# Up projection: products on TensorE, and casts and subtractions of left forms, chained in program order

## The chip, the cores and the metric

The kernel runs on one core of a Trainium2 chip. The metric is the device time of one execution in microseconds (us). The engines are named as in the profile: PE is TensorE, DVE is VectorE, ACT is ScalarE, POOL is GpSimd, and SP is the engine that issues most transfers.

## The reference

One layer of a decoder trunk with 1024 tokens and a model width of 1024. Only its last part, the gated MLP, touches the change:

```
def conv_gated_ffn(h, w_up, conv_w, conv_b, w_down):
    u, v = jnp.split(h @ w_up, 2, axis=-1)
    u = lax.conv_general_dilated(u, conv_w[:, None, :], window_strides=(1,),
                                 padding=[(CONV_W - 1, 0)], ...) + conv_b
    return (jax.nn.silu(u) * v) @ w_down
```

`h` is the normalised activation (1024 x 1024), `w_up` is 1024 x 5632, so `u` and `v` have 2816 columns each; the convolution along the tokens is causal and has width 3. All data are float32.

## The kernel before

The product `h @ w_up` is computed by tiles of 128 columns. Tile f of `u` and tile f of `v` (f = 0 to 21) make one **pair**. Within a pair the kernel uses a scheme of seven products in place of eight: the two column tiles, the two halves of the inner dimension (512 each) and the two halves of the tokens (512 each) make a 2 x 2 block product, done as Winograd's variant of Strassen's scheme. The left factors are weights or sums of weights (A11, A12, A22 and S1 to S4, called **left forms**), the right factors are activations or sums of them (B11, B21, B22 and T1 to T4), made once in `trunk`.

Each product is computed in split precision. A factor is held as a high part, cast to a reduced format, and a low part, the difference. `left` makes a form: POOL adds weights where the form is a sum (L1308), ACT casts the high part (L1315), and DVE and POOL in turn subtract for the low part (L1316). The form's tile has one of two tags in turn, with two buffers each, so the cast of a form can run only when the product four forms earlier has ended. `prod` issues the product: twelve matmuls of 128 x 512, for each of four inner blocks high x high, high x low, low x high (L1323).

In a pair, the products accumulate into a bank a (`ps_a`), a bank b (`ps_b2`, in the profile `ps_b`), and one tile `cd` of two banks (`ps_cd`), whose halves are c and d. In the code's order: A11 x B11 into a, S2 x T2 into b, S3 x T3 into c, S1 x T1 into d, A12 x B21 into a, A22 x T4 into c, S4 x B22 into d. DVE adds the partial sums as they come (L1384 u2 = b + s1, L1386 u3 = c + u2, L1388 the second half of vt = d + u3, L1393 the first half of vt = c + u2, L1395 the second half of u = d + u2), and then convolution, silu and the gate follow, called the y chain here: L1397 on ACT, L1398 and L1399 on DVE, the silu L1400 on ACT, L1401 on DVE, and then L1404 (even f) or L1411 (odd f) on DVE. PSUM holds two `ps_cd` tiles, one `ps_b` for each of two pairs, and two `ps_a`.

For the first six pairs the two products into bank a are computed ahead, by `ahead`, and their results are kept in DRAM (`part_dram`); these pairs have five products left. `ahead` starts while `trunk` still transposes activations, so that the first products stand among the transposes (L1254) of the last token blocks and the token-major matmuls (L1099).

The order of instructions on each engine is set by a scheduler, which works from dependencies and a timing estimate of its own. Where the code demands no order, two products, of one pair or of two neighbouring pairs, may be interleaved. `tc.issue_after(x)` adds the demand that what is issued inside it stands behind instruction x.

Of the kernel before, what the change touches and what calls it, by code (L numbers as in the profile page):

```python
# [12 lines left out]
F32 = mybir.dt.float32  # L13
# [4 lines left out]
ALU = mybir.AluOpType  # L18
# [78 lines left out]
class K:  # L97
# [1197 lines left out]
    def left(self, r1, r2, which, sp):  # L1295

        nc = self.nc
        V, A, G = nc.vector, nc.scalar, nc.gpsimd
        q = {f"A{n}{k + 1}": r[:, 4 * k:4 * k + 4, :] for n, r in ((1, r1), (2, r2)) if r is not None for k in range(2)}
        sums = {"S1": ("A21", "A22", ALU.add), "S2": ("S1", "A11", ALU.subtract), "S3": ("A11", "A21", ALU.subtract),  # L1300
                "S4": ("A12", "S2", ALU.subtract)}

        def get(n):
            if n not in q:
                a, b, op = sums[n]
                a, b = get(a), get(b)
                q[n] = sp.tile([P, 4, P], F32, tag=n, name=n, bufs=2 if n in ("S1", "S2") else 1)
                G.tensor_tensor(out=q[n], in0=a, in1=b, op=op)  # L1308
            return q[n]

        for n in which:
            x = get(n)
            self.nform = getattr(self, "nform", 0) + 1
            f = self.wp.tile([P, 2, 4, P], F32R, tag=("whi", "wlo")[self.nform % 2], name="wf")
            A.copy(out=f[:, 0], in_=x)  # L1315
            (V if self.nform % 2 else G).tensor_tensor(out=f[:, 1], in0=x, in1=f[:, 0].bitcast(F32), op=ALU.subtract)  # L1316
            yield f

    def prod(self, ps, f, x, start, stop):
        n = 0  # L1320
        for k in range(4):
            for a, b in ((0, 0), (0, 1), (1, 0)):
                self.nc.tensor.matmul(ps, lhsT=f[:, a, k, :], rhs=x[b][:, k, :], start=(start and n == 0), stop=(stop and n == 11),  # L1323
                                      skip_group_check=not start)
                n += 1

    def ffn_up(self, X, act, sums, part, spill):

# [302 lines left out]
```

## Time and profile before

| | us |
|---|---|
| time, median of 3 runs | 2422.68 |
| its lowest and highest run | 2419.61, 2427.7 |
| the profiled execution's own time | 2418.76 |
| its span | 2417.0 |
| PE busy in the span | 2312.8 (96%) |
| DVE busy | 1373.9 (57%) |
| ACT busy | 908.9 (38%) |
| POOL busy | 695.2 (29%) |

The span runs from the first to the last instruction of the profiled execution, 1.8 us less than its time. Positions in the rows are microseconds from the start of the span. The up projection's products lie between 1700 and 2192 us. The busy time of an engine counts time in which it works on an instruction, waits not included; the wait in brackets behind a row of the timeline is the idle time of the engine just before the instruction, with what ended it.

### The profile page before, as it was taken

Reading aid. Unit: us, or ns where it says so; the run is one execution under the profiler, and the core shown is the slowest. Engines: PE = TensorE matmul, PEld = TensorE weight load, DVE = VectorE, ACT = ScalarE, POOL = GpSimd, SP = SyncE. Lnnn points to the kernel's source line nnn. Section 1 sums busy time; section 2 is a strip of 40 time slices with the busy share of each in tenths; the row PEclk is TensorE's granted clock in tenths of the full one; section 3 lists DMA queues with packets and bytes.
Section 4 is the critical chain, followed back from the end, with each engine's and each line's share of the span. In section 5 each row is a group of like instructions: output and inputs, shape, how many; then the busy total and the mean of one; then the engine's idle time right before and its main releaser. Section 6 shows DMA issues by size and latency. Waiting matters only on the chain. (4 is left out here: it accounts for less than half of the span.)

```text
span 2417.0 us, 34889 instructions
## 1 busy us (share of the span) xinstructions
PE 2312.8 (96%) x13988; PEld 1887.5 (78%) x13988; DVE 1373.9 (57%) x2098; ACT 908.9 (38%) x1430; POOL 695.2 (29%) x580
## 2 busy tenths in 40 slices
PE   7999999899999999999999999999898999998998
PEld 7877768686778787888878778888676888886886
DVE  6446374757424557454564464545547656667775
ACT  6542213131314435344442233443333333334443
POOL 1011001010111333333132440141456666551041
PEclk9999999999999999999999999999999999999999
DMA  8653312121222111111103662224243322238333
GB/s 302 221 176 125 92 58 97 58 92 45 76 70 81 53 53 37 35 60 54 44 27 121 215 213 96 96 88 135 106 165 135 111 94 105 105 142 306 97 96 122
DMA packets 110930, 266.14 MB, mean 110 GB/s; under 512 B 27248, under 2 KB 31984, under 8 KB 110768
## 3 DMA queue, kind: packets, MB, share of 16 engines
q1 hardware_dynamic: 108656, 258.25, 31.9%
q0 software_dynamic: 1248, 4.46, 0.5%
q8 instruction: 110, 1.80, 0.3%
q10 hardware_dynamic: 864, 1.20, 0.1%
q14 instruction: 52, 0.43, 0.1%
HBM read 194.40 MB, written 69.47 MB: 109 GB/s over the span
## 5 line engine op out<-in xcount | busy, mean ns | idle before, releaser
L155 PE MATMUL ps_d<-hThi,whi 128*128 128x512 f32 x1056 | 425.9, 404 | 2.0 <-DVE Ktt L261 1.6
L157 PE MATMUL ps_d<-hTlo,whi 128*128 128x512 f32 x1056 | 424.2, 402 | 0.0
L159 PE MATMUL ps_d<-hThi,wlo 128*128 128x512 f32 x1056 | 424.1, 402 | 0.0
L140 ACT CAST whi<-raw 128x1024 fp32r<-128x1024 f32 (+1 forms) x170 | 167.2, 989 | 331.4 <-PE ps_d L157 155.4
L143 DVE TENSOR_TENSOR wlo<-raw,whi 128x1024 fp32r<-128x1024 f32 (+1 forms) x125 | 156.9, 1262 | 138.2 <-ACT whi L140 138.2
L155 PEld LDWEIGHTS ps_d<-hThi,whi 128*128 128x128 f32 x1056 | 199.9, 189 | 44.5 <-issue 3.2
L157 PEld LDWEIGHTS ps_d<-hTlo,whi 128*128 128x128 f32 x1056 | 199.9, 189 | 42.8 <-issue 4.6
L159 PEld LDWEIGHTS ps_d<-hThi,wlo 128*128 128x128 f32 x1056 | 199.7, 189 | 42.7 <-issue 4.2
L143 POOL TENSOR_TENSOR wlo<-raw,whi 128x1024 fp32r<-128x1024 f32 (+1 forms) x45 | 96.8, 2150 | 433.1 <-ACT whi L140 388.4
L1490 PE MATMUL ps_dn<-wd,ap 128*128 128x512 f32 x924 | 213.2, 393 | 7.1 <-ACT wd L1466 6.7
L1490 PEld LDWEIGHTS ps_dn<-wd,ap 128*128 128x128 f32 x924 | 175.1, 190 | 45.2 <-ACT wd L1466 7.1
L1315 ACT CAST wf<-S 128x512 fp32r<-128x512 f32 x88 | 54.7, 622 | 165.0 <-PE ps_cd L1323 76.5
L1466 ACT CAST ap<-acr 128x512 fp32r<-128x512 f32 x77 | 47.9, 623 | 104.2 <-PE ps_dn L1490 93.2
L1467 DVE TENSOR_TENSOR ap<-acr,ap 128x512 fp32r<-128x512 f32 x77 | 61.4, 799 | 41.4 <-ACT ap L1466 40.6
L745 DVE CUSTOM_DVE_ANT_0 a_p<-ps_s,a_bias 128x512 f32<-128x512 f32 (+3 forms) x96 | 51.7, 553 | 50.3 <-PE ps_s L743 45.0
L159 PE MATMUL ps_d<-ohi,wlo 128*128 128x512 f32 x192 | 75.9, 395 | 3.3 <-DVE wlo L143 3.3
L1316 POOL TENSOR_TENSOR wf<-S,wf 128x512 fp32r<-128x512 f32 x44 | 62.0, 1409 | 56.1 <-ACT wf L1315 56.1
L755 ACT ACTIVATE a_p<-a_p,a_nm 128x128 f32<-128x128 f32 (+7 forms) x64 | 49.2, 770 | 75.2 <-POOL a_nm L751 57.8
L157 PE MATMUL ps_d<-olo,whi 128*128 128x512 f32 x192 | 75.8, 395 | 0.0
L155 PE MATMUL ps_d<-ohi,whi 128*128 128x512 f32 x192 | 75.8, 395 | 0.0
L1113 POOL TENSOR_SCALAR ms<-ms 128x1 f32<-128x1 f32 x30 | 11.1, 371 | 224.0 <-ACT xn L1112 146.1
L1308 POOL TENSOR_TENSOR S<-raw 128x512 f32<-128x512 f32 x44 | 58.9, 1341 | 35.6 <-DVE wf L1316 21.8
(436 smaller groups left out, 5386.3 us busy)
## 6 DMA issues: line engine op xcount, KB each, us to landing
raw<-t_in SPq DMA_DIRECT2D x66, 512.0 KB, 3.6
raw<-t_up SPq DMA_DIRECT2D x50, 512.0 KB, 3.5
th_dram<-th SPq DMA_DIRECT2D x24, 512.0 KB, 2.8
mth<-th_dram SPq DMA_DIRECT2D x24, 512.0 KB, 3.7
wdr<-ffn_w_down SPq DMA_DIRECT2D x44, 256.0 KB, 5.2
acr<-act_dram SPq DMA_DIRECT2D x44, 256.0 KB, 2.7
act_dram<-y SPq DMA_DIRECT2D x20, 512.0 KB, 2.6
acr<-sums_dram SPq DMA_DIRECT2D x33, 256.0 KB, 2.6
```

Source lines behind the costliest of these rows:

```text
L140: nc.scalar.copy(out=hi, in_=raw)
L143: eng.tensor_tensor(out=lo, in0=raw, in1=hi.bitcast(F32), op=ALU.subtract)
L155: nc.tensor.matmul(o, lhsT=hi[:, k, :], rhs=xhi(k, h), start=(k == 0), stop=False)
L157: nc.tensor.matmul(o, lhsT=hi[:, k, :], rhs=xlo(k, h), start=False, stop=False)
L159: nc.tensor.matmul(o, lhsT=lo[:, k, :], rhs=xhi(k, h), start=False, stop=(k == nk - 1))
L745: V.tensor_tensor_reduce(out=p_[:, a:b], in0=ps[:, 0:b - a], in1=bias[:, 1024 - n + a:1024 - n + b], op0=ALU.add, op1=ALU.max, scale=1.0, ...
L755: A.activation(out=pr[c][:, 0:n], in_=pr[c][:, 0:n], func=AF.Exp, bias=nm[:, c:c + 1], accum_out=Z[:, c:c + 1])
L1308: G.tensor_tensor(out=q[n], in0=a, in1=b, op=op)
L1315: A.copy(out=f[:, 0], in_=x)
L1316: (V if self.nform % 2 else G).tensor_tensor(out=f[:, 1], in0=x, in1=f[:, 0].bitcast(F32), op=ALU.subtract)
L1467: V.tensor_tensor(out=t[:, 1], in0=z, in1=t[:, 0].bitcast(F32), op=ALU.subtract)
L1490: T.matmul(ps[t], lhsT=a[:, p, P * t:P * t + P], rhs=w[:, q, :], start=(not behind and j == 0 and n == 0), stop=(j == NJ - 1 and n == 2), ...
```

## The change

`prod` now issues all its twelve matmuls behind the last matmul of the product that the code issued before it, over all calls, so that products on PE stand in the code's order and none is interleaved with another. A new function `inorder` chains instructions of one kind: the casts of left forms on ACT ("A"), the subtractions on DVE (1) and those on POOL (0). The instructions themselves stay as they were. Lines of the changed kernel behind the edit carry higher numbers: the cast is L1316, the subtraction L1317, the matmuls L1332, and each line from L1338 of the old numbering on is 12 higher.

```diff
--- before.py
+++ after.py
@@ -1312,17 +1312,29 @@
             x = get(n)
             self.nform = getattr(self, "nform", 0) + 1
             f = self.wp.tile([P, 2, 4, P], F32R, tag=("whi", "wlo")[self.nform % 2], name="wf")
-            A.copy(out=f[:, 0], in_=x)
-            (V if self.nform % 2 else G).tensor_tensor(out=f[:, 1], in0=x, in1=f[:, 0].bitcast(F32), op=ALU.subtract)
+            e = self.nform % 2
+            self.inorder("A", lambda: A.copy(out=f[:, 0], in_=x))
+            self.inorder(e, lambda: (G, V)[e].tensor_tensor(out=f[:, 1], in0=x, in1=f[:, 0].bitcast(F32), op=ALU.subtract))
             yield f
 
+    def inorder(self, n, f):
+
+        last = self.__dict__.setdefault("kinds", {})
+        with self.tc.issue_after(last[n].ins) if n in last else ExitStack():
+            last[n] = f()
+
     def prod(self, ps, f, x, start, stop):
-        n = 0
-        for k in range(4):
-            for a, b in ((0, 0), (0, 1), (1, 0)):
-                self.nc.tensor.matmul(ps, lhsT=f[:, a, k, :], rhs=x[b][:, k, :], start=(start and n == 0), stop=(stop and n == 11),
-                                      skip_group_check=not start)
-                n += 1
+
+        with self.tc.issue_after(self.before) if self.before is not None else ExitStack():
+            n = 0
+            for k in range(4):
+                for a, b in ((0, 0), (0, 1), (1, 0)):
+                    i = self.nc.tensor.matmul(ps, lhsT=f[:, a, k, :], rhs=x[b][:, k, :], start=(start and n == 0),
+                                              stop=(stop and n == 11), skip_group_check=not start)
+                    n += 1
+        self.before = i.ins
+
+    before = None
 
     def ffn_up(self, X, act, sums, part, spill):
```

The first place is PE in one pair of seven products, whose tile is `ps_cd_16159`. These are rows of the order before; `ps_cd_16298`, `ps_b2_16297` and `ps_a_16278` belong to the next pair, and what stands in brackets is which engines the matmul waits for.

```order
L1323 MATMUL ps_cd_16159<-T3hi_14291,wf_16184 128x512
...
L1323 MATMUL ps_a_16139<-B21hi_13803,wf_16216 128x512 [waits Activation_49]
...
L1323 MATMUL ps_cd_16159<-T1hi_14150,wf_16200 128x512 [waits DVE_49]
...
L1323 MATMUL ps_b2_16297<-T2hi_14141,wf_16305 128x512 [waits Activation_49]
...
L1323 MATMUL ps_a_16278<-B11hi_13794,wf_16279 128x512 [waits Activation_49]
...
L1323 MATMUL ps_cd_16159<-T4hi_14159,wf_16232 128x512 [waits DVE_49]
...
L1323 MATMUL ps_cd_16298<-T3hi_14291,wf_16323 128x512 [waits Activation_49]
L1323 MATMUL ps_cd_16298<-T3lo_14292,wf_16323 128x512
L1323 MATMUL ps_cd_16159<-B22hi_14321,wf_16250 128x512 [waits DVE_49]
```

And these are the rows of the changed order for the same pair.

```order
L1332 MATMUL ps_cd_16159<-T3hi_14291,wf_16184 128x512
L1332 MATMUL ps_cd_16159<-T1hi_14150,wf_16200 128x512 [waits DVE_49,Activation_49]
...
L1332 MATMUL ps_a_16139<-B21hi_13803,wf_16216 128x512 [waits Activation_49]
...
L1332 MATMUL ps_cd_16159<-T4hi_14159,wf_16232 128x512 [waits DVE_49,Activation_49]
...
L1332 MATMUL ps_cd_16159<-T4hi_14159,wf_16232 128x512
L1332 MATMUL ps_cd_16159<-B22hi_14321,wf_16250 128x512 [waits DVE_49,Activation_49]
...
L1332 MATMUL ps_a_16278<-B11hi_13794,wf_16279 128x512 [waits Activation_49]
```

T1 stood behind B21 and now stands right behind T3; B22 stood behind products of the next pair and now stands right behind T4, and B21 has moved between T1 and T4.

The second place is DVE around the addition u3 of the same pair (L1386); `y_16119` and `vt_16010` belong to the pair before. First the order before.

```order
L1395 TENSOR_TENSOR u_14365<-ps_cd_16012,u2_16013 128x512
L1384 TENSOR_TENSOR u2_16160<-ps_b2_16158,s1_16155 128x512
L1398 SCALAR_TENSOR_TENSOR y_16119<-u_14365,par_70,y_16119 128x1024
L1386 TENSOR_TENSOR u3_16161<-ps_cd_16159,u2_16160 128x512
L1316 TENSOR_TENSOR wf_16250<-S4_16248,wf_16250 128x512
L1399 SCALAR_TENSOR_TENSOR y_16119<-u_14365,par_70,y_16119 128x1024
L1316 TENSOR_TENSOR wf_16305<-S2_16303,wf_16305 128x512
L1401 TENSOR_TENSOR y_16119<-y_16119,vt_16010 128x1024
L1388 TENSOR_TENSOR vt_16157<-ps_cd_16159,u3_16161 128x512
```

Then the changed order.

```order
L1407 TENSOR_TENSOR u_14365<-ps_cd_16012,u2_16013 128x512
L1410 SCALAR_TENSOR_TENSOR y_16119<-u_14365,par_70,y_16119 128x1024
L1411 SCALAR_TENSOR_TENSOR y_16119<-u_14365,par_70,y_16119 128x1024
L1317 TENSOR_TENSOR wf_16216<-raw_15988,wf_16216 128x512
L1396 TENSOR_TENSOR u2_16160<-ps_b2_16158,s1_16155 128x512
L1413 TENSOR_TENSOR y_16119<-y_16119,vt_16010 128x1024
L1423 TENSOR_TENSOR asum_16126<-y_16119,y_15980 128x512
L1398 TENSOR_TENSOR u3_16161<-ps_cd_16159,u2_16160 128x512
L1317 TENSOR_TENSOR wf_16250<-S4_16248,wf_16250 128x512
L1400 TENSOR_TENSOR vt_16157<-ps_cd_16159,u3_16161 128x512
```

The addition u3 (L1386, now L1398) stood between the two steps of the convolution of the pair before, and now stands behind the whole y chain of that pair.

The third place is PE in one of the first six pairs, whose tile is `ps_cd_15062`. Before:

```order
L1323 MATMUL ps_cd_15062<-T1hi_14150,wf_15103 128x512 [waits DVE_49]
...
L1323 MATMUL ps_cd_15170<-T3hi_14291,wf_15195 128x512 [waits Activation_49]
...
L1323 MATMUL ps_cd_15062<-T4hi_14159,wf_15119 128x512 [waits DVE_49]
...
L1323 MATMUL ps_cd_15170<-T3hi_14291,wf_15195 128x512 [waits DVE_49]
...
L1323 MATMUL ps_cd_15062<-B22hi_14321,wf_15137 128x512 [waits DVE_49]
```

After:

```order
L1332 MATMUL ps_cd_15062<-T3hi_14291,wf_15087 128x512 [waits Activation_49]
...
L1332 MATMUL ps_cd_15062<-T3hi_14291,wf_15087 128x512
L1332 MATMUL ps_cd_15062<-T1hi_14150,wf_15103 128x512 [waits DVE_49,Activation_49]
...
L1332 MATMUL ps_cd_15062<-T4hi_14159,wf_15119 128x512 [waits DVE_49,Activation_49]
...
L1332 MATMUL ps_cd_15062<-B22hi_14321,wf_15137 128x512 [waits DVE_49,Activation_49]
```

Products of the next pair (`ps_cd_15170`) no longer stand between those of this one; the four products of the tile now follow one another.

## Rows read from the trace of the kernel before

**Rows 1.** Busy time of each engine by stretch: start:end, length, PE, PEld, DVE, ACT, POOL, PE clock, DMA share, GB/s
```profile
1700.00:1771.80 71.80, 62.92 (x292) 50.88 (x292) 36.19 (x43) 28.22 (x53) 32.55 (x28) 0.93 0.43 146
1771.80:1904.30 132.50, 118.70 (x497) 92.42 (x496) 81.04 (x86) 44.24 (x61) 87.53 (x61) 0.99 0.39 133
1904.30:2158.00 253.70, 253.53 (x1112) 207.93 (x1111) 159.40 (x167) 101.62 (x147) 155.66 (x109) 1.00 0.26 94
```

**Rows 2.** Timeline of PE in a pair of seven: start, duration, instruction
```profile
1923.82 0.39 PE L1323 MATMUL ps_cd<-T1hi,wf 128*128 128x512 f32 x1
...
1926.54 0.39 PE L1323 MATMUL ps_b<-T2hi,wf 128*128 128x512 f32 x1
```

**Rows 3.** What PE waited for, 1771.8 to 1904.3: total us, times, longest
```profile
PE ps_b L1323 <- ACT wf L1315: 4.8, 5, 1.9
PE ps_cd L1323 <- ACT wf L1315: 3.1, 4, 0.9
PE ps_cd L1323 <- DVE u L1386: 2.2, 1, 2.2
PE ps_a L1323 <- ACT wf L1315: 1.5, 2, 0.8
```

**Rows 4.** Timeline of PE, first matmul of T3 in two of the first pairs
```profile
1805.48 0.50 PE L1323 MATMUL ps_cd<-T3hi,wf 128*128 128x512 f32 x1 [0.88 <-ACT wf L1315]
...
1855.06 0.50 PE L1323 MATMUL ps_cd<-T3hi,wf 128*128 128x512 f32 x1 [0.71 <-ACT wf L1315]
```

**Rows 5.** What PE waited for, 1904.3 to 2158
```profile
PE ps_b L1323 <- POOL wf L1316: 0.2, 1, 0.2
```

**Rows 6.** Timeline of DVE and PE around the first pair's T1
```profile
1779.24 0.68 DVE L1386 TENSOR_TENSOR u<-ps_cd,u 128x512 f32<-128x512 f32 x1
...
1780.07 0.47 PE L1323 MATMUL ps_cd<-T1hi,wf 128*128 128x512 f32 x1 [2.17 <-DVE u L1386]
```

**Rows 7.** Timeline of DVE and PE in the last pair
```profile
2172.15 0.68 DVE L1386 TENSOR_TENSOR u<-ps_cd,u 128x512 f32<-128x512 f32 x1
...
2177.76 0.68 DVE L1388 TENSOR_TENSOR vt<-ps_cd,u 128x512 f32<-128x512 f32 x1
...
2178.59 0.47 PE L1323 MATMUL ps_cd<-T4hi,wf 128*128 128x512 f32 x1 [2.69 <-DVE vt L1388]
...
2181.61 0.69 DVE L1393 TENSOR_TENSOR vt<-ps_cd,u 128x512 f32<-128x512 f32 x1 [0.83 <-PE ps_cd L1323]
...
2182.45 0.47 PE L1323 MATMUL ps_cd<-B22hi,wf 128*128 128x512 f32 x1 [0.87 <-DVE vt L1393]
```

**Rows 8.** Groups by line, 1904.3 to 2158, DVE and ACT: busy us, mean ns | idle before
```profile
L1401 DVE TENSOR_TENSOR y<-y,vt 128x1024 f32<-128x1024 f32 x14 | 25.0, 1784 | 7.9 <-ACT y L1400 7.9
L1399 DVE SCALAR_TENSOR_TENSOR y<-u,par,y 128x1024 f32<-128x1024 f32 x14 | 21.0, 1501 | 0.0
L1398 DVE SCALAR_TENSOR_TENSOR y<-u,par,y 128x1024 f32<-128x1024 f32 x13 | 16.7, 1285 | 4.6 <-ACT y L1397 4.1
...
L1395 DVE TENSOR_TENSOR u<-ps_cd,u 128x512 f32<-128x512 f32 x13 | 9.0, 693 | 37.9 <-PE ps_cd L1323 37.9
...
L1411 DVE TENSOR_TENSOR asum<-y 128x512 f32<-128x512 f32 x6 | 7.4, 1232 | 0.0
...
L1315 ACT CAST wf<-S 128x512 fp32r<-128x512 f32 x53 | 33.0, 623 | 95.5 <-PE ps_cd L1323 37.3 <-PE ps_b L1323 29.3 <-PE ps_a L1323 28.9
...
L1397 ACT ACTIVATE y<-u,par 128x1024 f32<-128x1024 f32 x13 | 16.2, 1247 | 1.6 <-DVE u L1395 0.9
L1400 ACT ACTIVATE y<-y 128x1024 f32<-128x1024 f32 x14 | 14.9, 1063 | 0.7 <-DVE y L1399 0.2
```

**Rows 9.** Timeline of PE before the first pair
```profile
1713.41 0.39 PE L1323 MATMUL ps_a<-B11hi,wf 128*128 128x512 f32 x1
...
1744.82 0.78 PE L1323 MATMUL ps_a<-B21hi,wf 128*128 128x512 f32 x1
```

**Rows 10.** Busy time by stretch, as rows 1, for four microseconds
```profile
1785.00:1789.00 4.00, 3.99 (x10) 3.12 (x11) 1.74 (x1) 0.48 (x1) 4.00 (x4) 0.57 0.31 52
```

## Prediction

> **What bounds the kernel now.** I began with the busy time by stretch [rows 1]. The change touches the up projection only, so the stretches to look at are the one in which the first products lie among the last transposes (1700 to 1771.8), the one of the first six pairs (1771.8 to 1904.3), and the one of the pairs with seven products (1904.3 to 2158). The reader is to see that TensorE (PE) is busy for 253.53 of 253.70 us in the third, and for only 118.70 of 132.50 us in the second. In the third nothing can be gained by any order; it can only be lost. The pace there is one product of twelve matmuls in 1926.54 − 1923.82 = 2.72 us [rows 2], which is 0.2267 us for a matmul and 19.04 us for a pair of seven.
>
> Second, what PE waits for. In the first pairs it waits for casts of left forms on ACT, 4.8 + 3.1 + 1.5 us, and once for 2.2 us for a sum on DVE [rows 3]; the first T3 products of the pairs stand 16.5 us apart (three periods between 1805.48 and 1855.06) [rows 4], where five products at full pace take 13.6. By the matmul count, 497 × 0.2267 = 112.7 us of the stretch's 132.5 are pace, so it loses 19.8 us. In the seven-product pairs the whole list of waits is 0.2 us [rows 5].
>
> Third, what the waiting rows say of the two halves of `ps_cd`. T1 writes the second half (d), which nobody reads at that time; u3 = c + u2 reads the first half. Yet T1's first matmul started at 1780.07 after an idle 2.17 us put down to u3, which ran from 1779.24 for 0.68 [rows 6]. At the end of the stage the same shows twice [rows 7]: T4, which writes c, started at 2178.59, right after the addition that read d (2177.76 + 0.68 = 2178.44), though u3, the last reader of c, had ended at 2172.83. B22, which writes d, started at 2182.45, after the addition that read c (2181.61 + 0.69 = 2182.30). So **the program waits for the tile, not for the half**: T1 waits for u3, T4 for vt(d), B22 for vt(c), each of them an addition that can begin only when the product before it in this tile has ended. Before, other products stand between, and cover these waits.
>
> By the Trainium skill, page "PSUM — Partial Sum Buffer", section "PSUM bank collisions raise a hardware error", it is enough to guard PSUM by bank and quadrant, and a matmul next to a reader is to target a different bank. By that rule T1 would not wait for u3 here. The trace does not agree that this program waits so, by the 2.17 us and by 2178.59; what the rule would give is the first rival.
>
> **The price of one uncovered wait.** T4's first matmul at 2178.59 and B22's at 2182.45 are 3.86 us apart, where a product takes 2.72: 1.14 us for the last matmul's way out, the addition of 0.69, the hand-over, and the slower first matmul. This is the least that two products in one `ps_cd` cost when they are neighbours and DVE is free.
>
> **The change part by part.** The numbers of instructions stay the same, and no DMA is added. The chains only order: products on PE, casts on ACT, subtractions on DVE and POOL.
>
> *Pairs of seven, f = 6 to 20 (15 pairs).* In the new order T3 and T1 are neighbours, then B21, then T4 and B22 as neighbours. B21 (2.72 us) covers T4's wait for vt(d). T4 to B22 costs 1.14. T3 to T1 costs more, since u3 now stands on DVE behind the whole y chain of the pair before: from the end of B22 run the addition L1395 0.69, the ACT convolution 1.25, L1398 1.29, L1399 1.50, silu 1.06, L1401 1.78 [rows 8], then the half subtraction 0.68 for even f (taken as u3's, the same shape) or L1411's 1.23 for odd f, and u3 0.68. That is 8.93 or 9.48; with six hand-overs of some 0.12 (an estimate from 2178.44 to 2178.59 and from 1779.92 to 1780.07, which give 0.15, taken a little less) 9.6 or 10.2. B11, T2 and T3 take 3 × 2.72 = 8.16, so PE stands 1.5 or 2.0 us, and I take 1.85 with part of the slow start. Behind the waiting T1 stand all later products, and on ACT the casts that need a buffer which those products free; the three products of lead carry them. Together 3.0 a pair, 15 × 3.0 = **+45**. The lower bound is 2 × 1.14 = 2.28 a pair, +34: the chain is faster than I think and u3 is only just uncovered. The upper bound is another subtraction of 0.69 in front of u3, 3.7 a pair, +55. In the third stretch DVE is busy for 159.4 of 253.7 us and ACT for 101.6, 12.0 and 7.6 us a pair [rows 1], so neither becomes a bound by its work; only the latency of the chain counts.
>
> *First six pairs.* Without B11 and B21, T3, T1, T4 and B22 are all neighbours: three waits a pair, 18 in all. T4 to B22 is 1.14. Here u3 stands on DVE behind L1399: 0.69 + 1.25 + 1.29 + u2 0.69 (as L1395, the same shape) + 1.50, at times a subtraction 0.69, with hand-overs 5.8 to 6.5 from B22's end, while T2 and T3 end at 5.44. So T3 to T1 is 1.2 to 1.9, taken 1.5. vt(d) then stands behind L1401 and the half subtraction or L1411, which I take as 1.4 for T1 to T4. Sum 4.04 a pair, 24.2 for six. Against it the 19.8 us which this stretch loses now go: the casts waited because products of the next pair, interleaved with those of this one, held both buffers of a form; in strict order a form is prepared three products (8.2 us) ahead of its use, and the cast (0.62) with its subtraction fits into that. If they all go, **+4.4**; bounds 0 (18 × 1.14 = 20.5, about what is lost now) and +10 (some cast waits stay).
>
> *Before the first pair.* Before, a B11 product lies among the last token-major matmuls (1713.41) and four B11 products fill PE while activations are transposed; in the new order the first B21, which needs its transposed activations, stops what follows, so two products (24 matmuls, 5.4 us) move from under the transposes to behind them. The chain on DVE and ACT that ends there starts one product, 2.7 us, earlier. The first B21 started at 1744.82 [rows 9]. 5.4 − 2.7 = **+2.7**; bounds 0 (the whole is hidden by the chain's earlier start twice over) and +5.4 (none of it is given back).
>
> *The last pair.* Now it pays 2.69 + 0.87 in the two waits of [rows 7]; after, B21 covers T4, but T1 and B22 pay as in the other pairs: **+1**, bounds −2 and +5 (u3 behind a subtraction of the down projection's weights, which waits for a transfer).
>
> *Casts and subtractions in order.* For themselves I take **0**: they cost when a cast stands behind one whose input is late, by nearest row the longest wait for a cast, 1.9 us [rows 3]; 8.2 us of products ahead hide that. Without that cover it is a wait of 1.9 in a pair, inside the upper bounds above.
>
> **Sum.** 45 + 4.4 + 2.7 + 1 = 53 us. The profiled execution took 2418.76, so 2472 by it; it lies 3.9 us below the median of the runs shown (2422.68), against which the same sum gives 2476. I say 2474. Lower bounds together: 34 + 0 + 0 − 2 = 32, 2451; upper: 55 + 10 + 5.4 + 5 = 75, 2498.
>
> **The rivals.**
> 1. *The halves are independent after all* (the rule named above): then no neighbour waits, the sevens stay at full pace, and the cast waits of the first pairs go, 4.8 + 3.1 + 1.5 + 2.2 = 11.6 us, less the 2.7 at the start: 2418.8 − 8.9 = 2410 by the profiled run, 2414 by the median. This is the one on the other side; it decides if T1's first matmul waits for no addition. For it speaks that the idle rows are inferred from the last semaphore event; against it, three starts within 0.15 us of the end of an addition in the other half.
> 2. *The clock falls too.* After the two idle times of 2.17 and 1.94 us within 8 us, the granted clock was 0.57 from 1785 to 1789, and ten matmuls took 4.0 us instead of 2.27 [rows 10]: 1.73 lost. If every one of 21 pairs drew such a fall, +36 to my sum: 2510. Against it: the idle times I expect are mostly shorter than these two and 8 us apart, and single waits of 0.7 to 0.9 us per pair went with a clock of 0.99 over the stretch [rows 1, 4].
> 3. *The waits are hidden in part*, because DVE takes u3 sooner than its place suggests, or B22 finds vt(c) done: half of the sevens' cost, 2452 or less. Against it: an engine's order is fixed, and in the new order u3 stands behind L1411 or the half subtraction.
>
> **Chances.** My forecast (2452 to 2500) 0.84; rival 1 0.06; rival 2, above 2500, 0.06; rival 3, below 2452 and still slower, 0.04. A measurement of this kernel can tell about 0.3%, 7.3 us. Rival 1 lies at its edge, so it gives faster 0.04 and same 0.02; a little of rival 3 ends there too, so same is 0.03; slower 0.93. The range is 2452 to 2500: the bounds of the terms, and the lower part of rival 2.
>
> **What would show it.** In the changed kernel's sevens the list of waits should show two rows, T1 for u3 (L1398 in the new numbering, some 1.9 us for each of 15) and B22 for vt (L1405, 0.9), some 40 us of idle PE; the period of a pair should be 22.0 instead of 19.04; the cast waits of the first pairs should nearly vanish and three DVE waits a pair stand in their place, with a period of about 17.6. Wrong would be: PE without waits in the sevens (rival 1), a granted clock under 0.95 there (rival 2), or casts waiting in the place of additions.

## The result, and the profile after

The changed kernel takes 2501.89 us (median of 4 runs, 2497.97 to 2506.2) where the kernel before takes 2421.59 beside it: 1.0332 times, 95% interval 1.0311 to 1.0354. It is slower, as forecast, but by 80 us and not by 51 to 53, and it lies 1.9 us above the range. The profiled execution took 2497.97, with a span of 2496.0.

What PE waited for from 1700 to 2300 us, in the changed kernel (total us, times, longest):

```profile
PE ps_cd L1332 <- DVE u L1398: 48.3, 22, 3.9
PE ps_cd L1332 <- DVE vt L1405: 19.3, 22, 0.9
...
PE ps_cd L1332 <- DVE vt L1400: 6.7, 6, 1.6
```

Every one of the 22 pairs now waits for u3 (L1398) before T1 and for vt (L1405) before B22, and the six first pairs wait for vt (L1400) before T4 as well. The cast waits of [rows 3] are gone. The busy time by stretch, first pairs and pairs of seven (columns as [rows 1]):

```profile
1776.60:1881.10 104.50, 86.07 (x361) 65.98 (x360) 60.90 (x67) 31.75 (x43) 66.14 (x47) 1.00 0.40 132
1881.10:2239.80 358.70, 307.71 (x1262) 244.48 (x1261) 182.72 (x187) 112.70 (x165) 195.88 (x126) 0.96 0.26 82
```

Where PE stood still for 0.2 us in [rows 1], it is idle for 51 of 358.7 us, and the mean granted clock is 0.96 and not 1.00. Two pairs on PE's timeline:

```profile
2143.17 0.47 PE L1332 MATMUL ps_cd<-B22hi,wf 128*128 128x512 f32 x1 [0.87 <-DVE vt L1405]
...
2156.55 0.69 PE L1332 MATMUL ps_cd<-T1hi,wf 128*128 128x512 f32 x1 [2.22 <-DVE u L1398]
...
2167.46 0.47 PE L1332 MATMUL ps_cd<-B22hi,wf 128*128 128x512 f32 x1 [0.87 <-DVE vt L1405]
...
2181.58 0.47 PE L1332 MATMUL ps_cd<-T1hi,wf 128*128 128x512 f32 x1 [2.97 <-DVE u L1398]
...
2190.89 0.47 PE L1332 MATMUL ps_cd<-B22hi,wf 128*128 128x512 f32 x1 [0.88 <-DVE vt L1405]
```

T1's wait is 2.22 and 2.97 us in turn (2.92 in f = 6 and 1.58 in f = 20). From T1 to B22 stand three products, 9.31 us in the second of the two pairs and 10.91 in the first, and the difference is the clock (columns as before, the first 4 us of T1's product in each):

```profile
2156.50:2160.50 4.00, 3.95 (x10) 3.14 (x11) 0.00 (x0) 0.00 (x0) 1.70 (x2) 0.57 0.76 237
2181.50:2185.50 4.00, 3.92 (x17) 3.28 (x18) 1.93 (x2) 0.62 (x1) 3.78 (x4) 1.00 0.96 298
```

At a granted clock of 0.57 ten matmuls fit into 4 us, at 1.00 seventeen. 9 of the 15 pairs f = 6 to 20 show this fall, with 10.78 to 10.92 us from T1 to B22; the other six show 9.29 to 9.32.

Why T1 waits longer than forecast is on DVE. The chain that ends in u3, in the pair of the first two rows above:

```profile
2146.21 0.69 DVE L1407 TENSOR_TENSOR u<-ps_cd,u 128x512 f32<-128x512 f32 x1 [3.18 <-PE ps_cd L1332]
...
2148.35 1.66 DVE L1410 SCALAR_TENSOR_TENSOR y<-u,par,y 128x1024 f32<-128x1024 f32 x1 [0.79 <-ACT y L1409]
2150.05 2.20 DVE L1411 SCALAR_TENSOR_TENSOR y<-u,par,y 128x1024 f32<-128x1024 f32 x1
...
2153.38 1.22 DVE L1413 TENSOR_TENSOR y<-y,vt 128x1024 f32<-128x1024 f32 x1 [0.53 <-ACT y L1412]
2154.52 0.68 DVE L1317 TENSOR_TENSOR wf<-raw,wf 128x512 fp32r<-128x512 f32 x1
2155.12 0.68 DVE L1416 TENSOR_TENSOR y<-y 128x512 f32<-128x512 f32 x1
2155.72 0.68 DVE L1398 TENSOR_TENSOR u<-ps_cd,u 128x512 f32<-128x512 f32 x1
```

The same chain in the pair of the third and fourth row, from the second convolution step on, with the silu on ACT:

```profile
2173.86 2.20 DVE L1411 SCALAR_TENSOR_TENSOR y<-u,par,y 128x1024 f32<-128x1024 f32 x1
2175.99 1.78 DVE L1317 TENSOR_TENSOR wf<-raw,wf 128x512 fp32r<-128x512 f32 x1
2177.69 0.68 DVE L1396 TENSOR_TENSOR u<-ps_b,s 128x512 f32<-128x512 f32 x1
2178.29 1.81 DVE L1413 TENSOR_TENSOR y<-y,vt 128x1024 f32<-128x1024 f32 x1
2180.14 0.69 DVE L1423 TENSOR_TENSOR asum<-y 128x512 f32<-128x512 f32 x1
2180.75 0.68 DVE L1398 TENSOR_TENSOR u<-ps_cd,u 128x512 f32<-128x512 f32 x1
```

```profile
2176.10 1.06 ACT L1412 ACTIVATE y<-y 128x1024 f32<-128x1024 f32 x1 [1.79 <-DVE y L1411]
```

From the start of the addition on B22 (L1407, at 2146.21 and 2170.49) to T1's first matmul pass 10.3 and 11.1 us, where the sum gave 9.6 and 10.2. In the first chain the convolution steps take 1.66 and 2.20 us, the gate product (L1413) only 1.22, and a subtraction for a left form (L1317) stands between the gate product and the half subtraction. In the second the silu ends at 2177.16, but the gate product begins at 2178.29, 1.13 us later, because a subtraction of 1.78 us and u2 (L1396) stand in front of it on DVE. The two kinds of pair take turns. The groups by line of the pairs of seven (busy us, mean ns | idle before) show the two convolution steps longer than in [rows 8], 2140 ns for 1501 and 1459 for 1285 in the mean:

```profile
L1411 DVE SCALAR_TENSOR_TENSOR y<-u,par,y 128x1024 f32<-128x1024 f32 x15 | 32.1, 2140 | 0.5
...
L1410 DVE SCALAR_TENSOR_TENSOR y<-u,par,y 128x1024 f32<-128x1024 f32 x15 | 21.9, 1459 | 16.4 <-ACT y L1409 16.4
```

### The profile page after: what moved, and what is told of

Read it like the earlier page. It is cut to its first block, busy times and chain, and to the rows that moved or that the text cites. A ratio compares the mean times of both kernels' runs of the same rounds, so it can differ in the third digit from the quotient of the medians.

```text
span 2496.0 us, 34992 instructions
## 1 busy us (share of the span) xinstructions
PE 2331.8 (93%) x13988; PEld 1895.1 (76%) x13988; DVE 1373.8 (55%) x2098; ACT 907.9 (36%) x1430; POOL 709.8 (28%) x580
## 4 chain that ended last, share of the span: by engine, by line
PE 72%; DVE 14%; issue 4%; DMA 4%; ACT 4%; POOL 1%; SPq 0%; DVEq 0%; POOLq 0%; ACTq 0%
PE ps_tm L1099 10%; PE ps_d L157 10%; PE ps_d L155 10%; PE ps_d L159 10%; PE ps_cd L1332 8%; PE ps_dn L1502 7%; PE ps_a L1332 3%; PE ps_l L942 1%; PE ps_c L279 1%; DVE tmpa L453 1%; DVE tha L455 1%; PE ps_Y L279 1%; DVE y L1410 1%; DVE wlo L143 1%; PE ps_o L771 1%
## 5 line engine op out<-in xcount | busy, mean ns | idle before, releaser
L1332 PE MATMUL ps_cd<-T1hi,wf 128*128 128x512 f32 x176 | 71.2, 470 | 48.3 <-DVE u L1398 48.3
L1316 ACT CAST wf<-S 128x512 fp32r<-128x512 f32 x88 | 54.5, 621 | 142.6 <-PE ps_cd L1332 131.3
L1317 POOL TENSOR_TENSOR wf<-S,wf 128x512 fp32r<-128x512 f32 x44 | 61.3, 1394 | 125.9 <-ACT wf L1316 125.9
L1332 PEld LDWEIGHTS ps_cd<-T1hi,wf 128*128 128x128 f32 x176 | 40.4, 229 | 66.2 <-issue 47.4
L1316 ACT CAST wf<-raw 128x512 fp32r<-128x512 f32 x66 | 40.7, 618 | 120.2 <-PE ps_cd L1332 105.2
L1332 PE MATMUL ps_cd<-B22hi,wf 128*128 128x512 f32 x176 | 59.7, 400 | 19.3 <-DVE vt L1405 19.3
```

The source lines that it names most:

```text
L1316: self.inorder("A", lambda: A.copy(out=f[:, 0], in_=x))
L1317: self.inorder(e, lambda: (G, V)[e].tensor_tensor(out=f[:, 1], in0=x, in1=f[:, 0].bitcast(F32), op=ALU.subtract))
L1332: i = self.nc.tensor.matmul(ps, lhsT=f[:, a, k, :], rhs=x[b][:, k, :], start=(start and n == 0), stop=(stop and n == 11), skip_group_check ...
```

## The experiments

The kernel before ran beside each set: 2421.7 us with the first four, 2418.4 with the second four, 2416.4 with the last three. Ratios are against these.

### One half of the change at a time

Only casts and subtractions in order:

```diff
-        self.before = i.ins
+        self.before = None
```

> Only casts and subtractions of left forms are chained; products on PE are free again, and the scheduler interleaves them much as before. My theory (all the loss is in the order of products: neighbours in one ps_cd tile wait for the addition that reads its other half): within 10 us of the kernel before, 2412 to 2432, and the two DVE waits per pair of seven (T1 for u3, B22 for vt) absent. Rival (the chained casts and subtractions delay what stands behind them, the y chain on ACT and DVE above all): a good part of the 80 us stays, 2450 or more, with waits of PE for casts or of DVE for ACT.

Measured 2447.72 us, 1.0108 (1.0089 to 1.0127): 26 us slower and outside the 2412 to 2432 of my theory. From f = 8 to the last pair but one, neither of the two waits of the changed kernel is there. In their place the first B11 matmul of the next pair waits 0.71 to 0.75 us in each pair, and the period is 20.1 us, 1.07 above PE's pace; over these 13 pairs that is 14 of the 26 us. The rest lies at both ends: in f = 6 and 7, in the last pair, where T4 waited 5.28 us for vt, and before the first pair. PE and ACT at one of the B11 waits:

```profile
2061.22 0.39 PE L1332 MATMUL ps_cd<-T1hi,wf 128*128 128x512 f32 x1
2061.69 0.62 ACT L1316 CAST wf<-raw 128x512 fp32r<-128x512 f32 x1 [0.22 <-issue]
2062.36 0.50 PE L1332 MATMUL ps_a<-B11hi,wf 128*128 128x512 f32 x1 [0.75 <-ACT wf L1316]
```

T1's last matmul began at 2061.22 and ended at 2061.61; the cast began right behind it, and B11 right behind the cast. The form of the next A11 is the fourth behind S1's, so it takes the buffer that T1 frees, and the scheduler had put B11 right behind T1. So the chain of casts costs time where the products' order is not the casts' order; the next run tells what it costs where the two agree.

Only the products in order:

```diff
-            self.inorder("A", lambda: A.copy(out=f[:, 0], in_=x))
-            self.inorder(e, lambda: (G, V)[e].tensor_tensor(out=f[:, 1], ...))
+            A.copy(out=f[:, 0], in_=x)
+            (G, V)[e].tensor_tensor(out=f[:, 1], ...)
```

> Only the products are chained, casts and subtractions are free. My theory: as the changed kernel, 2490 to 2512, with T1 waiting for u3 in each pair (over 2 us) and B22 for vt (0.88 us). Rival (the chains on ACT and DVE make the y chain late, so that u3 is late): T1's wait falls to 0.9 to 1.5 us and the time to 2470 to 2485.

Measured 2498.59 us, 1.0317 (1.0292 to 1.0341), not to be told from the changed kernel's 1.0332. PE's waits for additions are also the same to the digit:

```profile
PE ps_cd L1332 <- DVE u L1398: 48.3, 22, 3.9
PE ps_cd L1332 <- DVE vt L1405: 19.3, 22, 0.9
```

So the order of products makes the loss, and once it is fixed the order of casts adds nothing that these runs can tell.

### Two tiles in place of one

```diff
-                cd = self.dps.tile([P, 1024], F32, tag="d", name="ps_cd")
-                c, d = cd[:, 0:512], cd[:, 512:1024]
+                c, d = (self.dps.tile([P, 1024], F32, tag="d", name=t)[:, 0:512] for t in ("ps_c1", "ps_d1"))
```

The same edit was made in the changed kernel and in the kernel before. Each pair now takes both buffers that two neighbouring pairs shared.

> The changed kernel, all chains kept, but c and d are two tiles (each the first bank of one of the two buffers) and no longer two halves of one. My theory (waits go by tile): T1 needs u3 no more, T4 finds it done, B22 finds vt(d) done; pairs of seven at 19.05 us instead of 23.9, first pairs near 13.6 instead of 17.4, so 2502 - 73 - 23 = 2406, within 2400 to 2420, faster than the kernel before. Rival (neighbours wait because DVE is late, whatever the tile): T1 or T4 still waits 1 to 3 us in each pair, 2460 or more.

> The kernel before, no chain, with c and d in two tiles. The scheduler then puts the pairs of seven in the code's order by itself from f = 8 on, and interleaves the first pairs a little. My theory: pairs of seven at PE's pace; first pairs lose less than the 21 us of before if casts come in time there, else the same; 2400 to 2422. Rival (interleaving by itself keeps PE busy and a pair in the code's order cannot): slower than before, 2440 or more.

With all chains 2402.94 us, 0.9921 (0.9899 to 0.9944); without a chain 2401.96, 0.9920 (0.9898 to 0.9942). Both are faster than both kernels. With all chains the products stand in the same order as in the changed kernel; only what they wait for differs. PE's waits in the kernel with chains, from 1772 to 2140 us, and the busy time of its first pairs and pairs of seven:

```profile
PE ps_d L1332 <- DVE vt L1399: 1.7, 3, 0.6
PE ps_d L1332 <- ACT wf L1316: 0.8, 1, 0.8
```

```profile
1772.00:1856.00 84.00, 81.55 (x357) 66.15 (x356) 71.19 (x65) 33.18 (x46) 76.02 (x47) 1.00 0.50 160
1880.00:2140.00 260.00, 260.00 (x1149) 215.36 (x1148) 174.84 (x172) 102.81 (x151) 178.89 (x115) 1.00 0.33 102
```

That is 2.5 us of waits in place of the changed kernel's 74, and no idle time in the pairs of seven. The first pairs run at 13.6 to 14.7 us a pair, and one cast wait of 0.8 is left of those in [rows 3]. In one pair of seven, T1's first matmul and u3 (here L1397):

```profile
1923.72 0.39 PE L1332 MATMUL ps_d<-T1hi,wf 128*128 128x512 f32 x1
```

```profile
1925.27 0.69 DVE L1397 TENSOR_TENSOR u<-ps_c,u 128x512 f32<-128x512 f32 x1
```

T1 begins 1.55 us before u3 does, right behind T3, and u3 reads c while T1 writes d. DVE is no quicker here: the second convolution step (L1410 in this run) takes 2.20 us in 14 of the 15 chains in front of the pairs f = 6 to 20, as in the changed kernel, and u3 still stands behind the y chain. Only it is no longer waited for.

Then the two tiles with chains in the pairs only, the products ahead left free:

```diff
-        self.before = i.ins
+        self.before = i.ins if self.chain else None
...
+                self.chain = True
```

> As the run with two tiles and all chains, but the products computed ahead are not chained, so that B11 products stand under the transposes again. Theory: the 4.8 us of the first part come back, 2403 - 5 = 2398, with first pairs near 14 us as there. Rival (the order of the first part costs nothing there, since what follows makes up for it): 2401 to 2405.

Measured 2402.06 us, 0.9936 (0.9921 to 0.9951), not to be told from the run with all chains. The B11 products stood under the transposes again, but the first T2 then waited 2.0 us for the transposed B22. The rival holds.

### u3 sooner, and POOL without sums

In the changed kernel, u3 ahead of the gate product of the pair before on DVE (the y chain's code moved behind u3's, and the gate product ordered behind it):

```diff
-                V.tensor_tensor(out=u3, in0=c, in1=u2, op=ALU.add)
+                i3 = V.tensor_tensor(out=u3, in0=c, in1=u2, op=ALU.add)
+                if later:
+                    later.pop()(i3)
...
-                V.tensor_tensor(out=y, in0=y, in1=vt, op=ALU.mult)
...
+                    with tc.issue_after(u3.ins) if u3 else ExitStack():
+                        V.tensor_tensor(out=y, in0=y, in1=vt, op=ALU.mult)
```

> The changed kernel, one tile cd and all chains kept, but on DVE u3 stands ahead of the gate product of the pair before (it was behind it and behind the half subtraction or the sum that follows). My theory: T1's wait in the pairs of seven falls from 2.2 to 3.0 us to the 0.88 of B22, which saves 15 x 1.64 + 3.1 = 28 us; and if the falls of the granted clock (9 of 15 pairs, 1.6 us each) come behind idle times of over 2 us, they go too, another 14: 2460. If the clock falls stay with idle times of 0.88, 2474. Rival (T1 is late for something else, its cast or the tile itself): T1's wait stays over 2 us, 2495 or more.

Measured 2462.55 us, 1.0183 (1.0166 to 1.02). Two products of one pair, and the busy time over the pairs of seven:

```profile
1976.11 0.47 PE L1332 MATMUL ps_cd<-T1hi,wf 128*128 128x512 f32 x1 [0.88 <-DVE u L1396]
...
1985.40 0.47 PE L1332 MATMUL ps_cd<-B22hi,wf 128*128 128x512 f32 x1 [0.88 <-DVE vt L1407]
```

```profile
1881.00:2210.00 329.00, 301.96 (x1299) 241.10 (x1297) 184.88 (x193) 117.22 (x171) 202.57 (x127) 1.00 0.28 94
```

In these pairs T1 waits 0.88 to 0.99 us, the clock is 1.00 throughout, and a pair takes 21.35 us (B22 of f = 5 at 1878.65, of f = 20 at 2198.95), 2.31 above PE's pace: twice the price of 1.14 that the prediction read from [rows 7]. T1's wait beyond that, and with it the falls of the clock, come from u3's place on DVE. The second convolution step still takes 2.20 us in 14 of the 15 chains in front of these pairs, so its length costs time only where u3 stands behind it and the gate product.

In the changed kernel, the sums left out:

```diff
-                a, b = get(a), get(b)
...
-                G.tensor_tensor(out=q[n], in0=a, in1=b, op=op)
+                q[n] = get(a)
```

> The changed kernel without the sums of weights on POOL (S1 to S4 are left out, their forms are made from A21, A21, A11, A12 instead, so the result is another function). Theory: POOL's work beside DVE stretches the convolution steps L1410 and L1411 (1.46 and 2.14 us, against 1.29 and 1.50 before), and that makes u3 late; without the sums L1411 falls to 1.5 or less, T1's wait by some 0.6 to 1.0 us a pair: 2485 to 2492, less if clock falls go as well. Rival (the durations are their own, or u3 is late for the casts on ACT): L1411 stays near 2.1 and the time within 5 us of 2502.

Measured 2470.14 us, 1.0217 (1.0201 to 1.0232), more than the theory asked for. In the pairs of seven the order on DVE is that of the changed kernel. Both convolution steps take 1285 ns, the gate product 1.22 us in every pair, and the subtraction in front of it 0.68 in place of 1.78; T1's wait falls to 1.16 and 1.58 us in turn, and none of the pairs f = 6 to 20 shows a fall of the clock:

```profile
L1408 DVE SCALAR_TENSOR_TENSOR y<-u,par,y 128x1024 f32<-128x1024 f32 x15 | 19.3, 1285 | 16.4 <-ACT y L1407 16.4
L1409 DVE SCALAR_TENSOR_TENSOR y<-u,par,y 128x1024 f32<-128x1024 f32 x15 | 19.3, 1285 | 0.5
```

```profile
2001.80 0.47 PE L1330 MATMUL ps_cd<-T1hi,wf 128*128 128x512 f32 x1 [1.16 <-DVE u L1396]
...
2023.81 0.47 PE L1330 MATMUL ps_cd<-T1hi,wf 128*128 128x512 f32 x1 [1.58 <-DVE u L1396]
```

### The first pairs, and a fifth form buffer

Chains in the products ahead and the first six pairs only:

```diff
-        self.before = i.ins
+        self.before = i.ins if self.chain else None
...
+                self.chain = True if f < ne else False
```

> All chains only in the products ahead and in the first six pairs; the pairs of seven are free. By the two traces the first part costs 4.8 and the six pairs 2.0, so 2421.6 + 7 = 2428, within 2422 to 2436. Rival (the first pairs' cast waits return something that the pairs of seven lose): below 2418, or over 2445 if a free pair behind chained ones loses as e1's did.

Measured 2428.59 us, 1.0037 (1.0023 to 1.0051), 10 us above its own before (6 to 12 by the interval), where the two terms say 7.

Five form buffers in turn:

```diff
-            f = self.wp.tile([P, 2, 4, P], F32R, tag=("whi", "wlo")[self.nform % 2], name="wf")
+            i = self.nform % 5
+            f = (self.wp if i else sp).tile([P, 2, 4, P], F32R, tag=("wf", "whi", "wlo", "whi", "wlo")[i], name="wf")
...
-                s1 = sp.tile([P, 512], F32, tag="s1", name=nm, bufs=3)
+                s1 = sp.tile([P, 512], F32, tag="s1", name=nm, bufs=2)
```

> The kernel before, no chain, with five form buffers used in turn and not four (one more tile of 4 KB; the s1 tile has two buffers for it and not three). The prediction said that the first pairs lose some 20 us because interleaved products hold the buffers of forms, so that a cast waits for the end of a product. If so, the cast waits of the first pairs (9 waits, 7.9 us, with their slow starts and the waits for subtractions behind them) go and the time falls to 2400 to 2410. Rival (one buffer more is used up by a scheduler that interleaves more): cast waits stay, within 7 us of 2421, or a new wait for additions between neighbours in cd.

> As the run in which only casts and subtractions are chained (2447.7), with five form buffers. There B11 of the next pair waits 0.73 us in each pair of seven, since its form takes the buffer that T1 has just freed. Theory: with a fifth buffer that wait goes, 15 x 1.0 = 15 us and some of the first pairs, 2415 to 2432. Rival (the chained casts are late for the y chain on ACT): no change, 2440 or more.

> Two tiles for c and d, no chain, five form buffers. In the run with two tiles and no chain PE waited 4.8 us in the up projection for u3 and for subtractions behind casts; if the fifth buffer takes these, 2398; if the scheduler's other order brings new waits, 2402 or more.

The kernel before becomes slower, 2432.14 us, 1.0062 (1.0046 to 1.0078); the one with only casts and subtractions chained stays near, 2436.76, 1.0081 (1.0065 to 1.0096); the two tiles without chains come to 2406.10, 0.9951 (0.9934 to 0.9967). All three theories miss; what came are the new waits between neighbours in `ps_cd` that the first rival named, and the 2402 or more of the third. In the first run, from 1771.8 to 1904.3:

```profile
PE ps_cd L1324 <- DVE vt L1389: 5.4, 4, 2.1
PE ps_b L1324 <- ACT wf L1316: 2.1, 3, 0.7
PE ps_cd L1324 <- DVE u L1387: 1.6, 1, 1.6
```

Cast waits fall from 9.4 us to some 3, but the scheduler, with a buffer more, interleaves otherwise, and T4 now waits for vt. In the second B11's wait is gone and T2 waits 0.71 to 0.76 us for its cast in most pairs. These runs changed the order, and the buffers of s1, along with the form buffer, so they do not tell what a fifth buffer is worth in one order.

## Why the prediction was right in its way and too small

**The waits by tile: right.** All neighbours in `ps_cd` wait, 22 + 22 + 6 times. Two tiles in the same order remove the waits, so the halves' common tile is shown as the cause, and the first rival (halves independent) is refuted as the program stands, and so is the third (waits hidden in part). By the Trainium skill, page "PSUM — Partial Sum Buffer", section "PSUM bank collisions raise a hardware error", a matmul may run beside a reader of another bank; with two tiles the trace agrees: u3 reads c at 1925.27 while T1 writes d, and PE is busy for 260.00 of 260.00 us. The rule held for the chip, and the wait for the whole tile was the program's.

**The price of 1.14: right.** B22's idle time is 0.87 to 0.88 in every pair, with a slow start of some 0.26 behind it, and the run with u3 sooner gives twice that to 0.03 us.

**The pairs of seven: the step that failed.** The term was 45 us and measured 73: 15 pairs from B22 of f = 5 (1878.52) to B22 of f = 20 (2237.20) took 358.7 us, against 15 × 19.04 = 285.6. T1's idle times sum to 37.9, B22's to 13.1, 30 slow starts of 0.26 to 7.8, and nine falls of the clock of some 1.57 to 14.1: 72.9. The period was 23.9 us and not 22.0. Two parts of the term were wrong.

The first is "PE stands 1.5 or 2.0 us, and I take 1.85": it stood 2.22 or 2.97 before the slow start. The path to u3 was the right one, but its sum took the durations of the old order and left out what else the new order puts on DVE. In the chain with the half subtraction, the convolution steps took 1.66 and 2.20 for 1.29 and 1.50, and a subtraction of 0.68 stood in the path, which the prediction had in its upper bound alone; the gate product took 1.22 for 1.78. In the other chain the second convolution step took 2.20, and the subtraction and u2, which stand in front of the gate product in the order shown with the change, held it for 1.13; the sum L1423 took 0.69 for 1.23. The hand-overs came to some 0.3 us and not to 0.72. Together that is 0.73 and 0.93 us more than forecast; parts of it that were too long hid others that were too short. The lengthening comes from POOL's sums: without them T1 waits 1.16 and 1.58, below the 1.5 and 2.0. The changed kernel shows the same in f = 20, where POOL has no sum to make beside the y chain: both steps take 1.28, the gate product 1.22, and T1 waits 1.58.

The second is that rival 2 was held apart from the sum, as a case of 6 in 100, with idle times "mostly shorter than these two". Of the 14 pairs in which T1 waited 2.2 us or more, 9 drew the fall, 14 us in all; the run with 0.88 to 0.99 and the run without sums (up to 1.58) drew none. The sign named for this rival, a granted clock under 0.95, did not show it: the mean over the stretch was 0.96. Without the falls, 59 us are left, above the term's upper bound of 55.

**First six pairs: right.** Measured 18.5 us of idle time and 18 slow starts of 0.26, 23.1 together (1776.63 to 1881.32, less 30 products), for 24.2 forecast, and a period of 17.4 us for 17.6. What they lost before was under-read: 492 matmuls (41 products) stand between the first T3 and T1 of f = 7, not the row's 497, so it was 21.0 and not 19.8. The net is +2.0 for +4.4.

**That the cast waits come from interleaving over few buffers: half shown.** Strict order removes them (0.8 us left with two tiles), and in the run with only forms chained each cast in front of a waiting B11 begins when the product that held its buffer ends. A fifth buffer did not remove them all under a free scheduler.

**Before the first pair: +4.8** (the first product of the pairs begins at 1776.63 and not at 1771.82), inside its bounds, +2.7 forecast: the first B21 began 1.25 us earlier (1743.57 for 1744.82) and not 2.7. **Last pair: +2.7** for +1. It loses 6.9 us, T1's wait of 3.94 and a fall of the clock in it, and lost 4.2 before. The +1 does not follow from the prediction's own figures, 3.0 for a pair after against 2.69 + 0.87 now, and that it has the right sign is luck. **Casts and subtractions in order: 0**, right where the products are ordered (1.0317 and 1.0332), but 26 us where they are not, which the prediction did not see.

The terms add up: the pairs of seven lost 1.9 us before, so they grew by 71.2, and 4.8 + 2.0 + 71.2 + 2.7, less 1.7 by which the part behind B22 of the last pair is shorter, are the 79.0 us between the two profiled spans.

## What to carry to other kernels

Before fixing an order by hand, ask which pairs of neighbours share a tile: in this program a wait for a tile covered both its banks, and what looks like an arbitrary interleaving may be what hides it. Split the tile first; in this kernel that gave 0.8% with either order. When a chain of durations is carried over to a new order, take for each instruction what it costs beside the neighbours that it will have there, add those that the new order puts in front of it, and price a fall of the clock as a part of the sum once idle times come near those that showed one.

## What was not expected of the hardware

The same convolution step on DVE (L1411) took 1285 ns with no sums on POOL and 2.20 us with them in 14 of 15 chains, in the same order on DVE, while u3, which reads one operand from PSUM, took 0.68 to 0.69 us in all the runs. By the Trainium skill, page "SBUF — State Buffer", section "Who interferes with whom", a DVE instruction with two SBUF inputs contends with a GpSimd instruction that reads SBUF, and one with at most one SBUF input, outside DVE's two-port modes, does not; these rows agree.

Idle times of 2.22 and 2.97 us before T1, with one of 0.88 before B22 in each pair, brought the granted clock to a mean of 0.57 over 4 us (the lower level, 1.2 GHz, for most of it) in 9 of 14 pairs, 1.6 us each time; idle times up to 1.58 in the same places brought it in none. Which of the pairs are hit, no run explains: the two lengths are hit about equally often, and the run with only the products chained, with the same idle times, shows the fall in 8 of these 14 pairs, of which three (f = 11, 16, 18) are not among the 9. It stays open. The last pair, where T1 waited 3.3 to 3.95 us, drew the fall in all four runs with T1 behind T3 in one tile throughout.
